# Sums of squares on VectorE in the first stage, and a reordered entry to the MLP

## The chip, the cores and the metric

The kernel runs on one core of a Trainium2 chip. Its five engines work beside each other, each through its own instructions in order: TensorE (PE; its weight loads are shown as PEld), VectorE (DVE), ScalarE (ACT), GpSimd (POOL) and SyncE (SP, which issues most DMAs). The metric is the device time of one execution in microseconds, as the median of several runs.

## The reference

One decoder layer over a sequence of 512 positions with a model width of 2048, in float32:

```python
a = rms_norm(h, norm_mix_pre)
z = a @ w_in          # recurrent branch, queries, keys, values, gates
y = concat([rms_norm(y_lru, gnorm_lru), rms_norm(y_nsa, gnorm_nsa)])
h = h + rms_norm(y @ w_out, norm_mix_post)
f = square(relu(rms_norm(h, norm_mlp_pre) @ mlp_w1)) @ mlp_w2
h = h + rms_norm(f, norm_mlp_post)
h = h + sigmoid(h @ ple_gate) * (p @ ple_proj)
```

The change touches two places: the first norm with the first products (the values and the gates), and the step from the mixer's output `h` into `mlp_w1`.

## The kernel before, in words

**Float32 products in three parts.** A matrix is split into a high part that TensorE multiplies exactly and a low part, the difference. ScalarE makes the high part and VectorE the low part, so each product is three matmuls (`mm3`): weight high with activation high, weight high with activation low, weight low with activation high. The weights come in strips of 128x512 (four tiles of 128x128). A strip's raw data lies in one of five `raw` buffers of two strips each, its high part is `shi` (ScalarE, L158) and its low part `slo` (VectorE, L159), in five buffers each. A raw buffer is free for SyncE's next load when its second `slo` is done. The activations' parts are `cx` or `cy`: two tiles (high, low) for each block of 128 channels.

**The order.** Work is a list of strips. `go()` walks through it: at strip j it fires the hooks of that place, splits strip j+4, and issues the 12 matmuls of strip j. `at(j, fn)` puts a hook at strip j, in quarters of a strip. So the order on every engine is written by hand, by the numbers in the tables, and each engine then waits for its data in that order. `store(dst, src, delay)` puts a DMA issue on ScalarE's queue `delay` strips later.

**The first stage** (`front`, 16 strips). Strip k holds the value weights of block k. For each of the 16 blocks of x, `x_step` splits the block (high on ScalarE and low on VectorE, L161 and L162), and `x_square` squares it on ScalarE (L601) and adds it into `msum`, on GpSimd (L605). At strip 6 `rms_a` reduces `msum` with 8 tiny matmuls on TensorE (L480) between strips 5 and 6. The gate weights are split into `gw` (L592, L593) ahead of block 1.

**The MLP's entry** (`back`). `b0` is the strip of four products of the last step (PLE), `bk = b0 + 4` the first of the MLP. The mixer's output lies in eight pairs `y[0]` to `y[7]` of two blocks each (128x1024). For pair i, `h1_a` multiplies by the norm and adds x (two VectorE instructions, L1432 and L1433), `h1_hi` makes the two high parts (ScalarE, L1440), `h1_lo` the two low parts (VectorE, L1443), `h1_sq` squares the pair into the tile that held x (ScalarE, L1449), `h1_add` adds the squares into `hs` (VectorE, L1453), which frees that tile for a later x, and `h1_e` scales the pair in place (ScalarE, L1456). `load_x` loads x for a pair; two tiles `xt` serve pairs 0, 1, 4, 5 and two tiles `xz` pairs 2, 3, 6, 7. The first four rows of `mlp_w1` run side by side (`add_plain`): 48 matmuls take blocks 0 to 3 for all four rows, then each row takes blocks 4 to 7 (one strip each), then 8 to 11, then 12 to 15. A pair's place is `b0 + HT[i]`, with its five steps at the offsets `HB`.

Of the kernel before, what the change touches and what calls it, by code (L numbers as in the profile page):

```python
# [11 lines left out]
AF = mybir.ActivationFunctionType  # L12
ALU = mybir.AluOpType
# [3 lines left out]
S = 512  # L17
# [17 lines left out]
NTAB = 1039  # L35
H = S // 2
PRIO = 20000
HT = (1.75, 2.75, 4, 4.25, 4.75, 8.5, 10.75, 12.25)
HB = (0, 0.5, 0.75, 1, 2)
HB1 = (0, 0.75, 1, 1.25, 2)  # L40
RMT = 16.5
WO = (-12, -7.75, -6.75, -5.75)
NPL = 12
# [60 lines left out]
GE = 8  # L104
# [18 lines left out]
def f32(ap):  # L123
    return ap.bitcast(F32)
# [14 lines left out]
class Build:  # L139
# [32 lines left out]
    def at(self, j, fn, *a):  # L172
        key = math.floor(4 * j + 0.5)
        assert self.now is None or key > self.now, (key, self.now)
        self.hooks.setdefault(key, []).append((fn, a))
# [385 lines left out]
    def front(self):  # L561
        nc, A, T, at = self.nc, self.A, self.T, self.at
        v, g, act, pe = nc.vector, nc.gpsimd, nc.scalar, nc.tensor
# [7 lines left out]
        gw = T["x2"].tile([P, KT, P], F32R, name="gw")  # L571
        sq_last = []
        wv = {}
# [6 lines left out]

        def load_wv(k):
            wv[k] = self.raw_tile()
            nc.sync.dma_start(wv[k], A["w_v"][k // 2])

        def load_gate():
            T["graw"] = self.raw_tile()
            nc.sync.dma_start(T["graw"][:, :768], A["w_gate"])
            g.memset(f32(gw), 0.0)

        def split_gate():  # L590
            src = T["graw"][:, :768].rearrange("p (k n) -> p k n", n=48)
# [7 lines left out]
        def x_square(k):  # L599
            sq = self.msum if k == 0 else T["x2"].tile([P, S], F32, tag="sq", name="sq", bufs=3)  # L600
            act.activation(sq, xs(k), AF.Square)  # L601
            if k == KT - 1:
                sq_last.append(sq)
            elif k:
                g.tensor_tensor(self.msum, self.msum, sq, op=ALU.add)  # L605

        def v_mm(j, q):
            if j == 0 and q == 0:
# [39 lines left out]


        self.msk = self.cp.tile([P, NB], F32, name="msk")  # L650
        at(-7, load_x, 0)
        at(-7, lambda: nc.sync.dma_start(self.vec, A["vecs"]))
        for i in range(8):
            at(-7 if i < 4 else 2 * i - 10, load_wv, 2 * i)
            if i == 0:
                at(-7, load_gate)
            for k in (2 * i + 1, 2 * i + 2):
                if k < KT:
                    at(-7 if i < 4 else -6, load_x, k)
# [3 lines left out]
        for k in range(KT):  # L663
            at(-3.75 + XS * (k - 1) if k else -5, x_step, k)
            at(XQ + XS * (k - 1), x_square, k)
            self.strips.append(Strip(lambda k=k: wv[k - k % 2][:, (k % 2) * 512:(k % 2 + 1) * 512], v_mm))
# [728 lines left out]
    def back(self):  # L1395
        nc, A, T, at = self.nc, self.A, self.T, self.at
        v, g, act = nc.vector, nc.gpsimd, nc.scalar
        V = self.vec

        b0 = len(self.strips)  # L1400
# [23 lines left out]
        def h1_a(i):  # L1424
            y, x, r = self.y[i], T["xt", i], T["Ro"]
            if i == 0:
                for a in range(2):
                    v.tensor_tensor(y[:, a], y[:, a], r, op=ALU.mult)
                    v.tensor_tensor(y[:, a], y[:, a], x[:, a], op=ALU.add)
                    h1_hi(a)  # L1430
            else:
                v.tensor_tensor(y, y, r.unsqueeze(1).to_broadcast([P, 2, S]), op=ALU.mult)  # L1432
                v.tensor_tensor(y, y, x, op=ALU.add)  # L1433
                if i > 1:
                    h1_hi(2 * i)
                    h1_hi(2 * i + 1)
            self.store(self.h1_d[2 * i:2 * i + 2].rearrange("a p n -> p a n"), y)

        def h1_hi(k):
            act.activation(up[k][:, 0], xs(k), AF.Copy, scale=V[:, V_MLPPRE + k:V_MLPPRE + k + 1])  # L1440
# [53 lines left out]
        bl = len(self.strips)  # L1494
        self.add_plain(bl, [A["mlp_w1"][m] for m in range(NPL - 4, NPL)], up, plain_a(NPL - 4), "Rm", (-8, -7, -6, -5))
        for i in range(KT // 2):
            j = b0 + HT[i]
            if i >= 4:
                at(b0 + HT[i - 4] + 2.25, load_x, 2 * i)
            if i == 1:  # L1500
                for a in range(2):
                    at(j + 0.5, h1_hi, 2 + a)
            for o, fn, k in zip(HB if i != 1 else HB1, (h1_a, h1_lo, h1_lo, h1_sq, h1_add), (i, 2 * i, 2 * i + 1, i, i)):
                at(j + o, fn, k)
            for a in range(2):
                at(j + GE, h1_e, 2 * i + a)
        at(bk + RMT, self.sqrt_table)
        at(bk + RMT, lambda: self.rms_a([T["hs"][:, 0], T["hs"][:, 1]], D, "m"))
        for i in range(KT // 2):
# [72 lines left out]
        for c in range(NCHUNK):  # L1582
            cb = len(self.strips)
            for k in range(FC):
                o = CU[k] if c == 0 else F1 + 4 * k if k < 8 else F2 + 0.4 * (k - 8)
# [80 lines left out]
        for i in range(KT // 2):  # L1666
            j = last + GT8[i]
# [109 lines left out]
```

## Time and profile before

| | |
|---|---|
| median of 3 runs | 2366.52 us (2366.48 to 2367.39) |
| the profiled execution's own time | 2364.17 us |
| its span in the trace | 2362.4 us |
| mean granted clock of TensorE | 0.997 |
| PE busy | 2316.7 us, 98% of the span |
| DVE, ACT, POOL busy | 59%, 44%, 5% |

The span runs from the first to the last instruction; 1.77 us of the profiled execution's time lie around it. The shares are means over stages with different limits; the two places of the change cover some 40 us and some 50 us of the span.

### The profile page before, as it was taken

The page shows a single profiled execution, that of the slowest core. Times are in us where ns is not written, and L with a number is a line of the kernel's source. Part 1 is how long each engine was busy: PE and PEld are TensorE (multiplying, and loading weights), DVE is VectorE, ACT ScalarE, POOL GpSimd, SP SyncE. Part 2 cuts the span into 40 slices and gives each one's busy share as a digit, 9 for nine tenths or more (in the row PEclk, how much of TensorE's full clock was granted, in tenths as well). Part 3 has the DMA queues.
Part 4 walks back from the last instruction along what each step waited for, and adds up shares of the span by engine and source line. Part 5 has one row for each costly group of instructions (what it writes and reads, how often), then busy time and mean ns, then how long its engine had stood idle before and what let it go on. Part 6 is the DMA issues. An engine that isn't in the chain of part 4 may idle for free.

```text
span 2362.4 us, 33256 instructions
## 1 busy us (share of the span) xinstructions
PE 2316.7 (98%) x12586; PEld 2004.2 (85%) x12586; DVE 1401.7 (59%) x2383; ACT 1039.6 (44%) x1927; POOL 108.5 (5%) x157
## 2 busy tenths in 40 slices
PE   7999999999999999999999999999999999999999
PEld 6788888787888778999999999888888888888887
DVE  6365665488746776888888888333333333334733
ACT  5354665387744563544444444333223223223422
POOL 4000000044410000000000000000000000000000
PEclk9999999999999999999999999999999999999999
DMA  5453232644234643433333335433333333224641
GB/s 190 155 179 121 96 110 103 174 124 122 99 116 134 234 149 107 143 132 130 128 130 127 134 125 184 155 116 134 116 116 132 110 115 134 98 99 134 221 145 69
DMA packets 113733, 315.59 MB, mean 134 GB/s; under 512 B 11459, under 2 KB 16835, under 8 KB 113573
## 3 DMA queue, kind: packets, MB, share of 16 engines
q1 hardware_dynamic: 94900, 275.13, 34.8%
q10 hardware_dynamic: 18672, 38.34, 4.6%
q8 instruction: 98, 1.61, 0.3%
q14 instruction: 63, 0.51, 0.1%
HBM read 270.37 MB, written 43.06 MB: 133 GB/s over the span
## 4 chain that ended last, share of the span: by engine, by line
PE 90%; DVE 4%; ACT 2%; DMA 2%; issue 1%; ACTq 0%; SPq 0%; POOL 0%; POOLq 0%; DVEq 0%
PE ps_mm L166 28%; PE ps_mm L168 27%; PE ps_mm L167 27%; PE ps_o L1301 1%; PE ps_t L1274 1%; DVE slo L159 1%; PE ps_s L1241 1%; DMA y<-in_xT_dram 1%; ACT shi L158 1%; PE ps_s L1242 0%; PE ps_mm L615 0%; ACT al_P L1254 0%; PE ps_mm L616 0%; PE ps_mm L614 0%; PE ps_t L480 0%
## 5 line engine op out<-in xcount | busy, mean ns | idle before, releaser
L159 DVE TENSOR_TENSOR slo<-raw,shi 128x512 fp32r<-128x512 f32 x808 | 558.7, 697 | 805.1 <-ACT shi L158 790.7
L158 ACT ACTIVATE shi<-raw 128x512 fp32r<-128x512 f32 x808 | 503.9, 629 | 912.9 <-PE ps_mm L167 804.6
L166 PE MATMUL ps_mm<-cx,shi 128*128 128x512 f32 (+1 forms) x1984 | 699.4, 353 | 3.8 <-ACT shi L158 1.9
L167 PE MATMUL ps_mm<-cx,shi 128*128 128x512 f32 (+1 forms) x1984 | 695.9, 351 | 3.4 <-DVE cx L1443 3.4
L168 PE MATMUL ps_mm<-cx,slo 128*128 128x512 f32 (+1 forms) x1984 | 696.1, 351 | 0.1
L166 PE MATMUL ps_mm<-cy,shi 128*128 128x512 f32 (+1 forms) x1536 | 544.0, 354 | 2.6 <-ACT shi L158 2.6
L167 PE MATMUL ps_mm<-cy,shi 128*128 128x512 f32 (+1 forms) x1536 | 543.3, 354 | 1.6 <-DVE cy L1443 1.6
L168 PE MATMUL ps_mm<-cy,slo 128*128 128x512 f32 (+1 forms) x1536 | 543.3, 354 | 0.6 <-DVE slo L159 0.6
L166 PEld LDWEIGHTS ps_mm<-cx,shi 128*128 128x128 f32 x1984 | 376.0, 189 | 52.6 <-ACT shi L158 3.1
L167 PEld LDWEIGHTS ps_mm<-cx,shi 128*128 128x128 f32 x1984 | 375.7, 189 | 51.8 <-DVE cx L1443 4.9
L168 PEld LDWEIGHTS ps_mm<-cx,slo 128*128 128x128 f32 x1984 | 375.5, 189 | 51.0 <-DVE slo L159 1.7
L166 PEld LDWEIGHTS ps_mm<-cy,shi 128*128 128x128 f32 x1536 | 290.8, 189 | 42.3 <-ACT shi L158 3.2
L167 PEld LDWEIGHTS ps_mm<-cy,shi 128*128 128x128 f32 x1536 | 290.9, 189 | 41.3 <-DVE cy L1443 2.4
L168 PEld LDWEIGHTS ps_mm<-cy,slo 128*128 128x128 f32 x1536 | 290.8, 189 | 41.0 <-DVE slo L159 1.2
L158 ACT ACTIVATE shi<-wsum 128x512 fp32r<-128x512 f32 x156 | 96.8, 628 | 124.0 <-PE ps_mm L167 73.4
L159 DVE TENSOR_TENSOR slo<-wsum,shi 128x512 fp32r<-128x512 f32 x156 | 106.3, 688 | 36.5 <-ACT shi L158 36.4
L1254 ACT ACTIVATE al_P<-al_P,ar_stm 128x512 f32<-128x512 f32 (+3 forms) x128 | 70.5, 555 | 13.7 <-DVE ar_stm L1249 13.3
L1264 POOL TENSOR_SCALAR al_P<-al_P,ar_sts 128x512 f32<-128x512 f32 (+3 forms) x128 | 71.9, 583 | 59.1 <-ACT al_ph L1286 28.7
L166 PE MATMUL ps_mm<-y,shi 128*128 128x256 f32 x208 | 58.3, 280 | 0.0
L167 PE MATMUL ps_mm<-y,shi 128*128 128x256 f32 x208 | 58.0, 279 | 0.0
L168 PE MATMUL ps_mm<-y,slo 128*128 128x256 f32 x208 | 58.0, 279 | 0.0
L1249 DVE CUSTOM_DVE_ANT_0 al_P<-ps_s,al_tb 128x512 f32<-128x512 f32 (+3 forms) x128 | 56.1, 483 | 2.7 <-POOL al_P L1264 1.6
(346 smaller groups left out, 1993.7 us busy)
## 6 DMA issues: line engine op xcount, KB each, us to landing
raw<-in_mlp_w_dram SPq DMA_DIRECT2D x256, 512.0 KB, 3.7
raw<-in_w_in_dram SPq DMA_DIRECT2D x64, 512.0 KB, 3.5
raw<-in_w_out_dram SPq DMA_DIRECT2D x32, 512.0 KB, 3.9
fk<-f_d SPq DMA_DIRECT2D x32, 512.0 KB, 4.9
raw<-in_ple_gate_dram SPq DMA_DIRECT2D x32, 512.0 KB, 4.1
f_d<-z ACTq DMA_DIRECT2D x26, 512.0 KB, 2.8
y<-in_xT_dram SPq DMA_DIRECT2D x16, 256.0 KB, 6.4
raw<-in_w_v_dram SPq DMA_DIRECT2D x8, 512.0 KB, 5.2
```

The lines of the kernel that those rows point to most:

```text
L158: nc.scalar.activation(hi, src, AF.Copy)
L159: (eng or nc.vector).tensor_tensor(lo, src, f32(hi), op=ALU.subtract)
L166: mm(ps, whi, ahi, start=start, stop=False)
L167: mm(ps, whi, alo, start=False, stop=False)
L168: mm(ps, wlo, ahi, start=False, stop=stop)
L1241: mm(ps[:, :n], lq, t["kh"][:, b, :n], start=True, stop=False)
L1249: v.tensor_tensor_reduce(out=PP[qt, b], in0=X["s", qt][b], in1=X["tb"][:, qt * P:], scale=1.0, scalar=3e38, op0=ALU.add, op1=ALU.min, accu ...
L1254: act.activation(PP[qt, b], PP[qt, b], AF.Exp, scale=-1.0, bias=st["mn"][:, qt, b:b + 1], accum_out=st["sm"][:, qt, b:b + 1])
L1264: pool.tensor_scalar(PP[qt, b], PP[qt, b], st["sm"][:, qt, b:b + 1], 1.0, op0=ALU.mult, op1=ALU.mult)
L1274: pe.transpose(pt[:, qt * P:(qt + 1) * P], PP[qt, b][:, kt * P:(kt + 1) * P], self.ident)
L1301: mm(po[:, :S - kt * P], vv[:, 0, b, :], y, start=False, stop=False)
```

## The change

In the first stage GpSimd's work goes away: the 14 adds into `msum` and the clearing of `gw` go to VectorE. A one-element activation is put ahead of ScalarE's first work. The first load of value weights is issued as two halves. At the MLP's entry each step of each pair has a table of its own (`HA_` for `h1_a`, `HH_` for the high parts, `HL_` for the low parts, `HS_` for the squares, `HD_` for their sums, `HX_` for the loads of x), in place of one place for each pair and common offsets; the stores of `h1` stay one strip behind, the fifth pair's one and a half.

```diff
-HT = (1.75, 2.75, 4, 4.25, 4.75, 8.5, 10.75, 12.25)
-HB = (0, 0.5, 0.75, 1, 2)
-HB1 = (0, 0.75, 1, 1.25, 2)
+HA_ = (1.75, 2.75, 3.75, 4.5, 4.75, 8.5, 10.5, 12.25)
+HH_ = (0, 3.25, 4.25, 4.75, 5.25, 9.25, 11.25, 13.25)
+HL_ = (2.25, 3.5, 4.25, 4.75, 5.5, 9.5, 11.5, 13.5)
+HS_ = (2.75, 4.25, 4.75, 5.25, 6.5, 10.25, 12.25, 14.25)
+HD_ = (0, 4.75, 6.25, 7.25, 14.5, 15, 15.5, 16)
+HX_ = (0, 0, 0, 0, 2.25, 5, 6.5, 7.5)
...
         def load_wv(k):
             wv[k] = self.raw_tile()
-            nc.sync.dma_start(wv[k], A["w_v"][k // 2])
+            for c in (slice(0, S), slice(S, 2 * S)) if k == 0 else (slice(0, 2 * S),):
+                nc.sync.dma_start(wv[k][:, c], A["w_v"][k // 2][:, c])
...
-            g.memset(f32(gw), 0.0)
...
-                g.tensor_tensor(self.msum, self.msum, sq, op=ALU.add)
+                v.tensor_tensor(self.msum, self.msum, sq, op=ALU.add)
...
+        act.activation(self.scrap, self.ones, AF.Copy)
+        v.memset(f32(gw), 0.0)
...
-                if i > 1:
-                    h1_hi(2 * i)
-                    h1_hi(2 * i + 1)
-            self.store(self.h1_d[2 * i:2 * i + 2].rearrange("a p n -> p a n"), y)
+            self.store(self.h1_d[2 * i:2 * i + 2].rearrange("a p n -> p a n"), y, 1 if i != 4 else 1.5)
...
         for i in range(KT // 2):
-            j = b0 + HT[i]
             if i >= 4:
-                at(b0 + HT[i - 4] + 2.25, load_x, 2 * i)
-            if i == 1:
-                for a in range(2):
-                    at(j + 0.5, h1_hi, 2 + a)
-            for o, fn, k in zip(HB if i != 1 else HB1, (h1_a, h1_lo, h1_lo, h1_sq, h1_add), (i, 2 * i, 2 * i + 1, i, i)):
-                at(j + o, fn, k)
+                at(b0 + HX_[i], load_x, 2 * i)
             for a in range(2):
-                at(j + GE, h1_e, 2 * i + a)
+                if i:
+                    at(b0 + HH_[i], h1_hi, 2 * i + a)
+                at(b0 + HL_[i] + (0.25 if i == 0 else 0) * a, h1_lo, 2 * i + a)
+                at(b0 + max(HA_[i] + GE, 15 if i > 4 else 0), h1_e, 2 * i + a)
+            at(b0 + HA_[i], h1_a, i)
+            at(b0 + HS_[i], h1_sq, i)
+            if i:
+                at(b0 + HD_[i], h1_add, i)
```

TensorE's instructions and their order are the same in both kernels. Three places show what moves on the engines that it waits for.

VectorE in the first stage before, from block 1's low part on (`cy` is the activation's low part, `slo` the strip's; the second, third and fourth `slo` are those of strips 1, 2 and 3):

```order
L162 SCALAR_TENSOR_TENSOR cy_104<-y0_95,vec_61,cy_104 128x512
L162 SCALAR_TENSOR_TENSOR cy_105<-y1_96,vec_61,cy_105 128x512
L159 TENSOR_TENSOR slo_169<-raw_123,shi_168 128x512
L162 SCALAR_TENSOR_TENSOR cy_106<-y1_96,vec_61,cy_106 128x512
L162 SCALAR_TENSOR_TENSOR cy_107<-y2_97,vec_61,cy_107 128x512
L162 SCALAR_TENSOR_TENSOR cy_108<-y2_97,vec_61,cy_108 128x512
L159 TENSOR_TENSOR slo_192<-raw_130,shi_191 128x512
```

The same stretch of VectorE in the changed kernel, up to strip 2's low part:

```order
L165 SCALAR_TENSOR_TENSOR cy_104<-y0_95,vec_61,cy_104 128x512
L608 TENSOR_TENSOR msum_66<-msum_66,sq_162 128x512
L165 SCALAR_TENSOR_TENSOR cy_105<-y1_96,vec_61,cy_105 128x512
L608 TENSOR_TENSOR msum_66<-msum_66,sq_167 128x512
L162 TENSOR_TENSOR slo_171<-raw_125,shi_170 128x512
L165 SCALAR_TENSOR_TENSOR cy_106<-y1_96,vec_61,cy_106 128x512
L608 TENSOR_TENSOR msum_66<-msum_66,sq_176 128x512
L165 SCALAR_TENSOR_TENSOR cy_107<-y2_97,vec_61,cy_107 128x512
L608 TENSOR_TENSOR msum_66<-msum_66,sq_181 128x512
L165 SCALAR_TENSOR_TENSOR cy_108<-y2_97,vec_61,cy_108 128x512
L608 TENSOR_TENSOR msum_66<-msum_66,sq_190 128x512
L162 TENSOR_TENSOR slo_194<-raw_132,shi_193 128x512
```

An add into `msum` now stands behind every block's low part, so each strip's low part has two or three more instructions ahead of it.

ScalarE at the MLP's entry before, from pair 2's high parts on (`y2_` to `y4_` are the pairs, `shi` a strip's high part, `ppo` an output of the PLE product, `xz` a square):

```order
L1440 ACTIVATE cy_7388<-y2_6705,vec_61 128x512
L1440 ACTIVATE cy_7389<-y2_6705,vec_61 128x512
L158 ACTIVATE shi_7538<-raw_7276 128x512
L1387 ACTIVATE ppo_7542<-ps_mm_7512 128x512
L1387 ACTIVATE ppo_7542<-ps_mm_7522 128x512
L1440 ACTIVATE cx_7390<-y3_6706,vec_61 128x512
L1440 ACTIVATE cx_7391<-y3_6706,vec_61 128x512
L1440 ACTIVATE cx_7392<-y4_6707,vec_61 128x512
L1440 ACTIVATE cx_7393<-y4_6707,vec_61 128x512
L1449 ACTIVATE xz_7412<-y2_6705 128x1024
L422 DMA h1_d_75<-y2_6705 128x2x512
L158 ACTIVATE shi_7617<-raw_7306 128x512
```

The same stretch of ScalarE in the changed kernel, from pair 2's high parts to the strip behind pair 4's:

```order
L1442 ACTIVATE cy_7390<-y2_6707,vec_61 128x512
L1442 ACTIVATE cy_7391<-y2_6707,vec_61 128x512
L1451 ACTIVATE xz_7414<-y2_6707 128x1024
L1442 ACTIVATE cx_7392<-y3_6708,vec_61 128x512
L1442 ACTIVATE cx_7393<-y3_6708,vec_61 128x512
L425 DMA h1_d_75<-y2_6707 128x2x512
L161 ACTIVATE shi_7617<-raw_7308 128x512
L1451 ACTIVATE xz_7416<-y3_6708 128x1024
L1442 ACTIVATE cx_7394<-y4_6709,vec_61 128x512
L1442 ACTIVATE cx_7395<-y4_6709,vec_61 128x512
L425 DMA h1_d_75<-y3_6708 128x2x512
L161 ACTIVATE shi_7629<-raw_7330 128x512
```

The high part of the second weight row's strip (`shi_7617`) now stands ahead of pair 4's high parts (the fifth pair's); the first row's strip and the last PLE output have moved ahead of pair 2, outside this piece.

VectorE at the MLP's entry before, from pair 3's update on:

```order
L1432 TENSOR_TENSOR y3_6706<-y3_6706,ps_t_7457 128x1024
L1433 TENSOR_TENSOR y3_6706<-y3_6706,xz_7414 128x1024
L1443 SCALAR_TENSOR_TENSOR cy_7388<-y2_6705,vec_61,cy_7388 128x512
L1453 TENSOR_TENSOR hs_7499<-hs_7499,xt_7316 128x1024
L1443 SCALAR_TENSOR_TENSOR cy_7389<-y2_6705,vec_61,cy_7389 128x512
L1443 SCALAR_TENSOR_TENSOR cx_7390<-y3_6706,vec_61,cx_7390 128x512
L1432 TENSOR_TENSOR y4_6707<-y4_6707,ps_t_7457 128x1024
L1433 TENSOR_TENSOR y4_6707<-y4_6707,xt_7536 128x1024
L1443 SCALAR_TENSOR_TENSOR cx_7391<-y3_6706,vec_61,cx_7391 128x512
L159 TENSOR_TENSOR slo_7618<-raw_7306,shi_7617 128x512
```

The same stretch of VectorE in the changed kernel:

```order
L1445 SCALAR_TENSOR_TENSOR cy_7390<-y2_6707,vec_61,cy_7390 128x512
L1445 SCALAR_TENSOR_TENSOR cy_7391<-y2_6707,vec_61,cy_7391 128x512
L1437 TENSOR_TENSOR y3_6708<-y3_6708,ps_t_7459 128x1024
L1438 TENSOR_TENSOR y3_6708<-y3_6708,xz_7416 128x1024
L1455 TENSOR_TENSOR hs_7503<-hs_7503,xt_7318 128x1024
L1445 SCALAR_TENSOR_TENSOR cx_7392<-y3_6708,vec_61,cx_7392 128x512
L1445 SCALAR_TENSOR_TENSOR cx_7393<-y3_6708,vec_61,cx_7393 128x512
L1437 TENSOR_TENSOR y4_6709<-y4_6709,ps_t_7459 128x1024
L1438 TENSOR_TENSOR y4_6709<-y4_6709,xt_7493 128x1024
L162 TENSOR_TENSOR slo_7618<-raw_7308,shi_7617 128x512
```

Each pair's two low parts now stand ahead of the next pair's update. Further back, the sums of squares of pairs 4 to 7 have moved behind pair 7's low parts.

## Rows read from the trace of the kernel before

**Rows 1.** The page's busy time, share of the span and instructions, by engine.

```profile
PE 2316.7 (98%) x12586; PEld 2004.2 (85%) x12586; DVE 1401.7 (59%) x2383; ACT 1039.6 (44%) x1927; POOL 108.5 (5%) x157
```

**Rows 2.** One stretch: its us, busy PE, PEld, DVE, ACT, POOL; clock, DMA share, GB/s.

```profile
30.00:34.00 4.00, 3.03 (x13) 2.53 (x14) 4.00 (x3) 1.55 (x3) 3.61 (x3) 1.00 0.01 2
```

**Rows 3.** Timeline of the first stage, VectorE and GpSimd: start, duration, instruction.

```profile
9.86 2.44 DVE L162 SCALAR_TENSOR_TENSOR cy<-y,vec,cy 128x512 fp32r<-128x512 f32 x2
10.17 23.60 POOL L605 TENSOR_TENSOR msum<-msum,sq 128x512 f32<-128x512 f32 x14 [7.64 <-ACT sq L601]
...
13.93 5.16 DVE L162 SCALAR_TENSOR_TENSOR cy<-y,vec,cy 128x512 fp32r<-128x512 f32 x3
...
34.24 0.68 DVE L159 TENSOR_TENSOR slo<-raw,shi 128x512 fp32r<-128x512 f32 x1
...
34.85 2.06 DVE L162 SCALAR_TENSOR_TENSOR cx<-y,vec,cx 128x512 fp32r<-128x512 f32 x3
```

**Rows 4.** Timeline of the first stage: the gate's load (SPq), ScalarE's start.

```profile
2.12 0.43 SPq L587 DMA_DIRECT2D raw<-in_w_gate_dram  x1
...
3.72 1.28 ACT L161 ACT_TABLE_LOAD   x1 [3.72 <-DMA vec<-in_vecs_dram]
...
8.11 0.84 ACT L592 ACTIVATE gw<-raw 128x768 fp32r<-128x768 f32 x1 [0.61 <-DMA raw<-in_w_gate_dram]
```

**Rows 5.** Timeline of the first stage, TensorE: second matmuls of strips 1, 2, 5, and after.

```profile
14.06 0.50 PE L615 MATMUL ps_mm<-slo,cy 128*128 128x512 f32 x1 [0.57 <-DVE slo L159]
...
20.81 0.50 PE L615 MATMUL ps_mm<-slo,cy 128*128 128x512 f32 x1 [3.29 <-DVE slo L159]
...
34.98 0.50 PE L615 MATMUL ps_mm<-slo,cy 128*128 128x512 f32 x1 [0.54 <-DVE slo L159]
...
38.06 0.28 PE L480 MATMUL ps_t<-ones,msum 128*128 128x1 f32 x2
...
39.77 0.48 PE L614 MATMUL ps_mm<-shi,cy 128*128 128x512 f32 x1
```

**Rows 6.** Timeline of TensorE at the MLP's entry.

```profile
809.32 0.39 PE L166 MATMUL ps_mm<-cy,shi 128*128 128x512 f32 x1
810.45 0.50 PE L167 MATMUL ps_mm<-cy,shi 128*128 128x512 f32 x1 [0.74 <-DVE cy L1443]
...
815.96 0.49 PE L167 MATMUL ps_mm<-cx,shi 128*128 128x512 f32 x1 [2.03 <-DVE cx L1443]
...
818.13 0.79 PE L166 MATMUL ps_mm<-cy,shi 128*128 128x512 f32 x1 [1.44 <-ACT shi L158]
...
831.77 0.40 PE L166 MATMUL ps_mm<-cx,shi 128*128 128x512 f32 x1
...
837.01 0.39 PE L168 MATMUL ps_mm<-cx,slo 128*128 128x512 f32 x1
...
847.57 0.50 PE L166 MATMUL ps_mm<-cx,shi 128*128 128x512 f32 x1
```

**Rows 7.** Timeline of VectorE at the MLP's entry.

```profile
803.50 1.22 DVE L1433 TENSOR_TENSOR y<-y,xz 128x1024 f32<-128x1024 f32 x1
806.65 0.69 DVE L159 TENSOR_TENSOR slo<-raw,shi 128x512 fp32r<-128x512 f32 x1 [1.93 <-ACT shi L158]
...
809.65 0.74 DVE L1443 SCALAR_TENSOR_TENSOR cy<-y,vec,cy 128x512 fp32r<-128x512 f32 x1
...
815.16 0.74 DVE L1443 SCALAR_TENSOR_TENSOR cx<-y,vec,cx 128x512 fp32r<-128x512 f32 x1
```

**Rows 8.** Timeline of ScalarE at the MLP's entry.

```profile
815.28 0.72 ACT L1440 ACTIVATE cx<-y,vec 128x512 fp32r<-128x512 f32 x1 [4.18 <-DVE y L1433]
...
816.52 1.04 ACT L1449 ACTIVATE xz<-y 128x1024 f32<-128x1024 f32 x1
817.47 0.61 ACT L158 ACTIVATE shi<-raw 128x512 fp32r<-128x512 f32 x1
...
839.44 1.32 ACT L1456 ACTIVATE y<-y,vec 128x512 f32<-128x512 f32 x2
```

## The prediction

> **What bounds the kernel now.** I read the page's busy shares first: TensorE works 98% of the span [rows 1], so the time is its work plus the stretches in which it waits, and a change that leaves its instructions alone can only take or add waits. The list of who waits for whom sends me to two places, the first 40 us and the MLP's entry, and I read both in the timelines, engine by engine.
>
> In the first stage TensorE waits for the strips' low parts, 0.57 us at strip 1, 3.29 at strip 2, 0.54 at strip 5 [rows 5]. VectorE makes them and has no gap. It is slow: three low parts of blocks take 5.16 us, 1.72 each, while GpSimd adds into `msum` from 10.17 to 33.77; as soon as GpSimd is done, three of the same take 2.06 us [rows 3]. GpSimd is the cause, not the loads: from 30 to 34 us the DMA share is 0.01 and VectorE still finishes three instructions in 4 us [rows 2].
>
> At the MLP's entry TensorE waits for the pairs' parts and for the strips. From 831.77 to 837.01 it issues 24 matmuls without a wait, 0.228 us apart. From 809.32 to 847.57 lie 108 issues (48 on blocks 4 to 7, 48 on 8 to 11, 12 on 12 to 15), which at that pace are 24.6 us; they take 38.25 [rows 6]. So 13.6 us are lost there. That is the ceiling of what an order can win at the entry.
>
> **The first stage, step by step.** Alone, VectorE starts a block's low part every 0.66 us ((2.06 - 0.74)/2; a single one lasts 0.74) and, behind a subtraction, the next instruction after 0.61 (34.24 to 34.85) [rows 3, 7]. The trace has no add of `msum` on VectorE. From below it costs 0.61, the pace of a subtraction of the same size; from above 1.69, the pace under GpSimd (1.72 less the tail of the last). I take 0.61, since GpSimd has nothing to do there any more. The chain starts at 9.86 as before, for the gate's split in front of it ends on a load (8.11) that the change doesn't hasten [rows 3, 4]. Adding up the new order (two block parts, two adds, `slo`; then three, three, `slo`; two, two, `slo`, three times; three, three, `slo`; one, `slo`) gives the ends of strips 1 to 7's low parts: 13.1, 17.5, 20.7, 23.8, 27.0, 31.4, 32.7. ScalarE's inputs are earlier everywhere, since it no longer waits for GpSimd to free a square.
>
> TensorE follows. From a strip's second matmul to the next strip's it needs 3.31 us (34.98 to 38.06 is 3.08, and one issue of 0.23) [rows 5]. Strip 1's second matmul goes at 13.15, strip 2's could at 16.46 and waits until 17.57, strips 3, 4, 5 go at 20.9, 24.2, 27.5 without a wait. The 8 reductions could start at 30.58, and the last add into `msum` ends at 30.8, so 30.83. Strip 6 starts 1.71 later, as before (38.06 to 39.77): 32.54 in place of 39.77, **7.2 us won**. Behind it the low part of strip 7 is there at 32.7 for 36.
>
> What else is in this stage costs nothing: the clearing of `gw` takes VectorE from nothing to at most the time of four subtractions (four times the elements), 2.7 us, at its start, where none of its inputs is there before 3.72, when ScalarE's first data lands [rows 4]. The early activation pulls the table load (1.28 us at 3.72) [rows 4] ahead of the first data; it brings up to 1.28 us for the first parts, which the gate's load takes back. The halved first load lets TensorE begin some tenths sooner, and strip 1's low part takes this back too; it puts one more issue (0.43 us) ahead of the gate's load [rows 4], so the term is 7.2 or, with that load 0.43 later, 6.8.
>
> **The entry, step by step.** Everything is the same up to pair 2's update, which ends at 804.72 [rows 7]. The first row's strip is now split ahead of that, so its low part no longer waits for ScalarE (1.93 us) [rows 7], and the low parts of blocks 4 and 5 follow at once, done at 806.3 and 806.9, where the first was done at 810.4 [rows 7]. The waits at them (the 0.74 of 810.45 is the first [rows 6]) go. An instruction on a whole pair lasts 1.22 [rows 7]; I count 1.25 where the next one needs its result and 1.14 where not, with the 0.08 of overlap that the block parts show (0.74 to 0.66). Pair 3's update takes 1.25 + 1.22 to 809.3, a sum of squares 1.14, then blocks 6 and 7 end at 811.1 and 811.8. TensorE comes to block 6 at 810.7: 0.25 us of wait there and none at block 7, where 2.03 were [rows 6].
>
> It reaches the second row at 812.4. Its high part was at 817.47, behind pair 4's parts (815.28) and a square [rows 8]; now it stands ahead of them, done at 811.2. What is late next is its low part, on VectorE behind pair 4's update: 811.7 + 2.5 = 814.1, and 0.69 for itself. The third matmul waits from 812.9 to 814.8, **1.9 us**. The next two rows' low parts end at 817.0 and 818.7 and are needed at 817.6 and 820.3. Pair 5's update is reached at 820.4, since its turn comes behind four strips' low parts and two sums; block 10 is done at 824.4, 0.3 late. Pair 6 is done at 831, three us early. Pair 7's update ends at 835.25, but ScalarE's queue then holds two pairs scaled in place (four activations, 0.6 apart) [rows 8] and a strip ahead of its high parts, so these end at 836.7 and the low parts at 837.4 and 838.1; TensorE is there at 835.3 and waits 1.5 and 0.55 us. With 0.1 us for each restart the waits come to 4.9 us, where 13.6 were: the second row's blocks 12 to 15 start at 838.8, not 847.57, **8.8 us won**.
>
> The queues it moves past: SyncE issues pair 4's x ahead of two stores, and the x tiles of pairs 6 and 7 come free at 818.1 and 819.8, behind the sums of squares, for use at 827.8 and 834.0; a load has 10 us there. The sums of pairs 4 to 7, now last, end at 844.1; the reduction that needs them comes behind two more rows and a strip, at 849. The stores of `h1` wait for updates that are done.
>
> The bounds of this term: nothing less than 13.6 - 4.9 if every instruction keeps its duration and no wait is missed. If the clock falls once as at 818.13, where a matmul takes 0.79 and others after a wait 0.50 [rows 6], the lower of the two levels (1.2 for 2.4 GHz) adds 0.228 us to each matmul, 1.4 to six of them; if pair 7's scalings find their turn late and the low parts of two pairs slip by a strip (2.7 us), the term is 5. From above, if all but the 1.9 is hidden, 11.
>
> **A rule that speaks against it.** VectorE is full in the first stage (4.00 of 4.00 us) [rows 2], and the change gives it 14 more instructions. The Trainium skill, Perfetto Trace Analysis, Optimizing Scalar/DVE Operations, says that where VectorE is saturated, moving work to ScalarE or even GpSimd may help, and adds that GpSimd shares a read port with it, so it might not. By its first half the 14 adds would lengthen the queue by 14 x 0.61 = 8.5 us and the change would lose there; by the rows a pace of 1.7 goes to 0.6 and the queue shortens. The trace agrees with the second half.
>
> **Rivals.** *The entry gives less*: one of the pairs' chains slips by a strip, or the clock falls: 7.2 + 5 won, 2354.3. For it speaks that ScalarE's and VectorE's queues there are added up from many durations; against it, that none of them changes. *The first stage gives less*: the gate's load comes much later than I think, or loads hold the blocks. With half of the 7.2, 2354.1. *The waits move on*, to work behind the entry, and less than 4.7 us remain: about 2364. Against it: TensorE's order is the same and what it waits for later hangs on work that moves with it. *Slower*: the slow pace isn't GpSimd's doing but that of these instructions in this stage, and stays at 1.69. Then 34 instructions (14 block parts, 14 adds, 6 low parts) end at 9.86 + 57.5 = 67.3, strip 6 starts 27.6 us later than now, and with 8.8 won the time is 2385. This decides from a pace of 1.14 us on (9.86 + 34 x 1.14 = 39.77 + 8.8). Against it: the pace changes within one instruction of GpSimd's end [rows 3].
>
> **How the numbers follow.** 7.2 + 8.8 = 16.0 us. The profiled execution's own time, 2364.17, has 1.77 around its span and would be 2348.2. The median of the runs shown is 2366.52, 2.35 above that execution, so I forecast 2350.5. Chances: the forecast, 2346 to 2353.5, 74 in 100; the entry gives less, 11; the first stage gives less, 9; the waits move on, 4; slower, 2. The range 2346 to 2356.5 takes in the two smaller gains. A measurement of this kernel can tell about 0.2% (4.7 us): faster by more than that 0.94, within it 0.04, slower 0.02.
>
> **What would show it.** Right: no GpSimd work before the attention; VectorE's `slo` instructions in the first stage 0.69 long, strip 2's wait near 1.1 us and strip 6's first matmul near 32.5; at the entry, with all times about 7 us earlier than my numbers, one wait of about 1.9 us at the second row's third matmul and one of about 2 at block 14, none at blocks 4 and 5. Wrong: instructions of VectorE still near 1.7 us in the first stage; the gate's split later than 9; a third large wait at the entry, for a load of x or for pair 5.

## The result, and the profile after

The changed kernel takes 2351.49 us (median of 6 runs, 2349.10 to 2353.67) where the kernel before takes 2366.50 (6 runs): a ratio of 0.9936 with a 95% interval of 0.9926 to 0.9946, 15.0 us less. The profiled execution took 2352.03 us, its span is 2350.2.

TensorE's work is the same, and the span is 12.2 us shorter; the page's first line, which answers to [rows 1], shows POOL 24 us lighter and DVE no heavier, though it has taken over 15 of POOL's instructions:

```profile
PE 2316.3 (99%) x12586; PEld 2006.0 (85%) x12586; DVE 1397.3 (59%) x2398; ACT 1039.8 (44%) x1928; POOL 84.2 (4%) x142
```

**The first stage.** VectorE's timeline in the changed kernel, which answers to [rows 3] (start, duration, instruction, and in brackets the idle time before it and who ended it; L165 is a block's low part, L608 an add into `msum`, L162 a strip's low part):

```profile
1.23 1.76 DVE L655 MEMSET gw<- 128x2048 f32 x1 [1.23 <-PEq L1775]
...
10.04 0.75 DVE L165 SCALAR_TENSOR_TENSOR cy<-y,vec,cy 128x512 fp32r<-128x512 f32 x1
10.70 0.68 DVE L608 TENSOR_TENSOR msum<-msum,sq 128x512 f32<-128x512 f32 x1
...
16.36 0.68 DVE L608 TENSOR_TENSOR msum<-msum,sq 128x512 f32<-128x512 f32 x1
16.96 0.68 DVE L162 TENSOR_TENSOR slo<-raw,shi 128x512 fp32r<-128x512 f32 x1
...
30.16 0.68 DVE L608 TENSOR_TENSOR msum<-msum,sq 128x512 f32<-128x512 f32 x1
```

An add lasts 0.68 us and the next instruction starts 0.60 after it; block parts are back at 0.74, where they took 1.72 [rows 3]. ScalarE's side answers to [rows 4]: the gate's weights arrive 0.18 later (8.29 in place of 8.11), so the chain starts at 10.04 and not at 9.86.

```profile
8.29 0.84 ACT L595 ACTIVATE gw<-raw 128x768 fp32r<-128x768 f32 x1 [2.00 <-DMA raw<-in_w_gate_dram]
```

TensorE's timeline there answers to [rows 5]. The kernel before had a fourth wait for a strip's low part, 1.62 us at strip 4, which the prediction's list leaves out. It also had a stretch at the lower clock in this stage, from 22.3 to 25.7, but that cost nothing: the next low part, strip 3's, was done only at 25.84, and TensorE took it at 25.89. From the kernel before, VectorE and TensorE:

```profile
24.07 1.77 DVE L159 TENSOR_TENSOR slo<-raw,shi 128x512 fp32r<-128x512 f32 x1
```

```profile
25.89 0.50 PE L615 MATMUL ps_mm<-slo,cy 128*128 128x512 f32 x1
...
30.97 0.50 PE L615 MATMUL ps_mm<-slo,cy 128*128 128x512 f32 x1 [1.62 <-DVE slo L159]
```

In the changed kernel two of these waits are left, 0.84 at strip 1 and 0.93 at strip 2; the reductions wait 0.37 for the last add, and strip 6 starts at 32.70 in place of 39.77:

```profile
13.31 0.50 PE L618 MATMUL ps_mm<-slo,cy 128*128 128x512 f32 x1 [0.84 <-DVE slo L162]
...
17.70 0.50 PE L618 MATMUL ps_mm<-slo,cy 128*128 128x512 f32 x1 [0.93 <-DVE slo L162]
...
30.89 0.38 PE L483 MATMUL ps_t<-ones,msum 128*128 128x1 f32 x2 [0.37 <-DVE msum L608]
...
32.70 0.48 PE L617 MATMUL ps_mm<-shi,cy 128*128 128x512 f32 x1
```

**The MLP's entry.** TensorE's timeline, which answers to [rows 6], from the first row's block 4 (804.81) to the second row's block 12 (835.15):

```profile
804.81 0.39 PE L169 MATMUL ps_mm<-cy,shi 128*128 128x512 f32 x1
...
806.68 0.50 PE L170 MATMUL ps_mm<-cx,shi 128*128 128x512 f32 x1
...
808.18 0.39 PE L170 MATMUL ps_mm<-cy,shi 128*128 128x512 f32 x1
810.33 0.50 PE L171 MATMUL ps_mm<-cy,slo 128*128 128x512 f32 x1 [1.76 <-DVE slo L162]
...
819.95 0.50 PE L170 MATMUL ps_mm<-cx,shi 128*128 128x512 f32 x1
...
830.55 0.39 PE L171 MATMUL ps_mm<-cx,slo 128*128 128x512 f32 x1
832.30 0.50 PE L169 MATMUL ps_mm<-cx,shi 128*128 128x512 f32 x1 [1.36 <-ACT cx L1442]
833.08 0.57 PE L170 MATMUL ps_mm<-cx,shi 128*128 128x512 f32 x1 [0.28 <-DVE cx L1445]
833.45 0.63 PE L171 MATMUL ps_mm<-cx,slo 128*128 128x512 f32 x1
833.87 0.63 PE L169 MATMUL ps_mm<-cx,shi 128*128 128x512 f32 x1
...
835.15 0.63 PE L169 MATMUL ps_mm<-cx,shi 128*128 128x512 f32 x1
```

Between the same two matmuls the kernel before took 38.25 us; here it is 30.34, 7.9 less. What is left of waits: 0.28 at block 6, 1.92 at the second row's third matmul (810.33 less 808.18, less an issue of 0.23), 0.19 at block 10, and at block 14 1.52 for the high and 0.55 for the low part. Then the matmuls come 0.43 apart instead of 0.23: the granted clock has fallen to its lower level behind the two waits, and eight matmuls pay 0.2 each, four of them up to block 12. The kernel before had a fall in this stretch too, behind 818.13 [rows 6]: to 821.15 seven issues take 3.02 us where 1.60 is their pace, and with 0.1 for the restart the fall took 1.3 us. So the waits alone, with their restarts, went from 12.3 us (13.6 less 1.3) to 4.9 (30.34 less 24.6 for the 108 issues, less 0.8).

Who is late at block 14 is seen on ScalarE and VectorE. Pair 7's update ends at 830.82, but ScalarE is still scaling two pairs in place (four activations, 2.55 us) and then splits a strip; pair 7's high parts start at 831.54:

```profile
828.57 2.55 ACT L1458 ACTIVATE y<-y,vec 128x512 f32<-128x512 f32 x4
...
831.02 0.61 ACT L161 ACTIVATE shi<-raw 128x512 fp32r<-128x512 f32 x1
831.54 1.32 ACT L1442 ACTIVATE cx<-y,vec 128x512 fp32r<-128x512 f32 x2
```

```profile
829.60 1.22 DVE L1438 TENSOR_TENSOR y<-y,xz 128x1024 f32<-128x1024 f32 x1
831.66 0.69 DVE L162 TENSOR_TENSOR slo<-raw,shi 128x512 fp32r<-128x512 f32 x1 [0.84 <-ACT shi L161]
832.28 1.41 DVE L1445 SCALAR_TENSOR_TENSOR cx<-y,vec,cx 128x512 fp32r<-128x512 f32 x2
```

**Where the rest went.** I cut each trace into four parts: up to strip 6's first matmul; the middle, up to the first matmul behind the reduction of the mixer's output; the entry, up to the first matmul behind the eight tiny ones of the MLP's norm; and the rest, which is 1503.1 to 1503.2 us in every trace but that of e6_scale_late (1504.6, with a fall of the clock at 941). What tells the other twelve apart lies in the first three parts. "Clock" is what the lower level took: 10 us times one minus the granted clock, summed over 10-us windows counted from the part's start. One fall mostly counts 1.7 there; where TensorE was waiting during part of it, it cost less.

| kernel | median us | ratio to before (95%) | strip 6 at | middle (clock) | entry (clock) |
|---|---|---|---|---|---|
| before | 2366.50 | | 39.77 | 751.6 (1.7) | 67.8 (1.7) |
| after | 2351.49 | 0.9936 (0.9926 to 0.9946) | 32.70 | 754.2 (5.1) | 60.3 (1.7) |
| e1_stage | 2360.20 | 0.9973 (0.9961 to 0.9984) | 32.38 | 754.4 (5.1) | 67.8 (3.4) |
| e2_entry | 2358.59 | 0.9968 (0.9955 to 0.9980) | 39.59 | 752.8 (3.4) | 60.3 (1.7) |
| e3_adds | 2359.58 | 0.9973 (0.9964 to 0.9982) | 32.71 | 753.2 (3.4) | 68.7 (3.4) |
| e4_extras | 2367.59 | 1.0005 (0.9996 to 1.0014) | 39.91 | 754.9 (5.1) | 67.8 (3.4) |
| e5_gp_reads | 2361.25 | 0.9978 (0.9968 to 0.9987) | 44.06 | 750.7 (1.7) | 60.3 (1.7) |
| e5_gp_writes | 2352.89 | 0.9940 (0.9927 to 0.9952) | 32.85 | 755.6 (6.8) | 60.3 (1.7) |
| e6_scale_late | 2350.15 | 0.9928 (0.9916 to 0.9940) | 32.80 | 753.2 (3.4) | 58.0 (0) |
| e7_pair4_first | 2349.94 | 0.9931 (0.9917 to 0.9944) | 33.07 | 754.3 (5.1) | 60.5 (1.7) |
| e8_again | 2352.43 | 0.9945 (0.9932 to 0.9959) | 33.14 | 756.1 (6.8) | 60.3 (1.7) |
| e9_scale_spread | 2347.99 | 0.9929 (0.9916 to 0.9941) | 32.62 | 751.6 (1.7) | 57.7 (1.7) |
| e10_spread_pair4 | 2353.69 | 0.9949 (0.9937 to 0.9962) | 32.87 | 757.2 (8.5) | 59.7 (1.7) |

The profiled execution won 7.1 in the first stage and 7.6 at the entry, and lost 2.6 in the middle, which the change doesn't touch. There its clock is lower in two places more than before's. Three windows of the changed kernel (busy us of PE, PEld, DVE, ACT, POOL, then the granted clock, DMA share, GB/s), with the one that answers to [rows 2] ahead:

```profile
30.00:34.00 4.00, 3.63 (x25) 2.99 (x24) 3.59 (x11) 0.98 (x3) 0.00 (x0) 1.00 0.08 22
...
150.00:160.00 10.00, 10.00 (x48) 8.42 (x47) 7.29 (x18) 6.45 (x14) 0.00 (x0) 0.83 0.39 135
...
460.00:470.00 10.00, 7.77 (x28) 5.86 (x29) 5.03 (x15) 2.57 (x4) 0.00 (x0) 0.83 0.50 150
...
640.00:650.00 10.00, 10.00 (x55) 8.72 (x54) 6.47 (x17) 5.98 (x17) 4.10 (x8) 0.89 0.16 58
```

In the kernel before, the same windows show 1.00, 1.00 and 0.83. Both kernels wait at all three places, for 1.7 to 3.2 us (the first is 3.19 us at 156.76 before and 2.94 at 149.38 after), so the length of the wait alone doesn't decide whether the clock falls.

### The profile page after: what moved, and what is told of

Read it like the earlier page. It is cut to its first block, busy times and chain, and to the rows that moved or that the text cites. A ratio compares the mean times of both kernels' runs of the same rounds, so it can differ in the third digit from the quotient of the medians.

```text
span 2350.2 us, 33252 instructions
## 1 busy us (share of the span) xinstructions
PE 2316.3 (99%) x12586; PEld 2006.0 (85%) x12586; DVE 1397.3 (59%) x2398; ACT 1039.8 (44%) x1928; POOL 84.2 (4%) x142
## 4 chain that ended last, share of the span: by engine, by line
PE 91%; DVE 4%; ACT 3%; DMA 1%; issue 1%; SPq 0%; ACTq 0%; POOL 0%; POOLq 0%; DVEq 0%
PE ps_mm L169 28%; PE ps_mm L171 28%; PE ps_mm L170 28%; PE ps_o L1306 1%; PE ps_t L1279 1%; DVE slo L162 1%; ACT shi L161 1%; PE ps_s L1246 1%; PE ps_s L1247 0%; ACT al_P L1259 0%; PE ps_t L483 0%; PE ps_mm L617 0%; PE ps_mm L619 0%; PE ps_mm L618 0%; DVE y L1438 0%
## 5 line engine op out<-in xcount | busy, mean ns | idle before, releaser
L162 DVE TENSOR_TENSOR slo<-raw,shi 128x512 fp32r<-128x512 f32 x808 | 554.3, 691 | 797.1 <-ACT shi L161 782.7
L162 DVE TENSOR_TENSOR slo<-wsum,shi 128x512 fp32r<-128x512 f32 x156 | 106.1, 687 | 36.8 <-ACT shi L161 36.7
```

What stands on the lines that cost most here:

```text
L162: (eng or nc.vector).tensor_tensor(lo, src, f32(hi), op=ALU.subtract)
```

## The experiments

**e1_stage and e2_entry: each half alone.** The first takes only these lines of the diff, the second all the others:

```diff
-            nc.sync.dma_start(wv[k], A["w_v"][k // 2])
+            for c in (slice(0, S), slice(S, 2 * S)) if k == 0 else (slice(0, 2 * S),):
+                nc.sync.dma_start(wv[k][:, c], A["w_v"][k // 2][:, c])
-            g.memset(f32(gw), 0.0)
-                g.tensor_tensor(self.msum, self.msum, sq, op=ALU.add)
+                v.tensor_tensor(self.msum, self.msum, sq, op=ALU.add)
+        act.activation(self.scrap, self.ones, AF.Copy)
+        v.memset(f32(gw), 0.0)
```

> The first stage's edits alone, the MLP's entry as before. My account (two independent terms): strip 6's first matmul near 32.7 us in place of 39.77, so 7.1 us won, about 2359.4; at the MLP's entry all of the old waits, 13.6 us. The rival, that the entry carries nearly all of the gain: under 3 us won, above 2363.

> The MLP entry's edits alone, the first stage as before, with GpSimd's adds. My account: 8.8 us won, less some 1.5 where the clock falls, so 2357.7 to 2359.5; strip 6's first matmul at 39.8; at the entry one wait of 1.8 us at the second row's third matmul and one of some 1.7 at block 14. The rival, that the first stage carries nearly all: under 3 us won.

Against the kernel before on the same chip (2366.18) the first won 6.0 us and the second 7.6. In the traces the first moves strip 6 to 32.38 and leaves the entry at 67.8; the second leaves strip 6 at 39.59 and has the changed kernel's entry, with its two waits (1.76 at the second row, 1.35 at block 14). Each half leaves the other's place as it was, and 13.6 for both is near the 15.0 of the change.

**e3_adds and e4_extras: the first stage taken apart.** The first moves only the 14 adds; the second does the rest of the stage's edits and leaves the adds on GpSimd.

```diff
-                g.tensor_tensor(self.msum, self.msum, sq, op=ALU.add)
+                v.tensor_tensor(self.msum, self.msum, sq, op=ALU.add)
```

> Only the 14 adds go from GpSimd to VectorE; the clearing of gw stays on GpSimd, no early activation, the first load in one piece. My account: VectorE's low parts 0.74 and 0.68 us long throughout, strip 6's first matmul between 32.4 and 32.8, 7.1 us won, 2359.4. The rival, that the earlier start (table load, half load) is needed too: one to two us less won, strip 6 near 34.

> The early activation, the load in halves and the clearing on VectorE, with the adds left on GpSimd. My account: TensorE begins near 6.3 instead of 7.6, and the time stays within 1 us of before (2366.5), since strip 1's low part waits for the gate's load and for VectorE at 1.7 us an instruction. The rival, that an earlier start is carried through: 1.2 us or more won.

The adds alone bring strip 6 to 32.71, and 6.6 us in the time; the other edits bring nothing that can be measured (e4_extras' median is 1.4 above before's on that chip, where I had said within 1, but its interval includes a ratio of 1). With the adds still on GpSimd VectorE stays slow, as e4_extras' timeline shows (three block parts in 5.16 us, a low part in 1.76):

```profile
12.38 1.76 DVE L159 TENSOR_TENSOR slo<-raw,shi 128x512 fp32r<-128x512 f32 x1
14.07 5.16 DVE L162 SCALAR_TENSOR_TENSOR cy<-y,vec,cy 128x512 fp32r<-128x512 f32 x3
```

**e5_gp_reads and e5_gp_writes: is it GpSimd's presence, or its reading?** To the changed kernel comes work on a tile that nobody uses, in the first 14 adds of GpSimd, which last 22.7 us in all, in the second 40 clearings, which last 23.3:

```diff
+        idle = self.sum_tile("idle")
+        g.memset(idle, 0.0)
+        for _ in range(14):
+            g.tensor_tensor(idle[:, :S], idle[:, :S], idle[:, S:], op=ALU.add)
```

```diff
+        idle = self.sum_tile("idle")
+        for _ in range(40):
+            g.memset(idle[:, :S], 0.0)
```

> The changed kernel with 14 adds of 128x512 on GpSimd over an unused tile, on which nothing waits. If reads by GpSimd hold VectorE up, the chain of msum having no part in it: about half of the adds run before 10 us, the rest at 1.7 us each beside VectorE's until some 22 us, VectorE's instructions are 1.6 to 1.8 us long until then, strip 6 starts near 40, and the time is 6 to 9 us above the changed kernel's. If it was the chain through msum (ScalarE waiting for GpSimd, GpSimd for ScalarE): VectorE at 0.7, the time of the changed kernel.

> The changed kernel with 40 clearings of an unused 128x512 tile on GpSimd from the start on, which only write. If GpSimd's reads are what holds VectorE up: VectorE's instructions stay at 0.68 to 0.75 us, strip 6's first matmul near 32.7, the time that of the changed kernel (2351.5, within 1.5). If any work of GpSimd holds it up: some of VectorE's instructions beyond 1 us, strip 6 after 35, 2354 or more.

Timelines of e5_gp_reads, GpSimd's and VectorE's: while GpSimd adds, VectorE's add takes 1.76 us, and the first instruction after it 0.74.

```profile
1.77 22.73 POOL L659 TENSOR_TENSOR idle<-idle 128x512 f32<-128x512 f32 x14
```

```profile
23.29 1.76 DVE L608 TENSOR_TENSOR msum<-msum,sq 128x512 f32<-128x512 f32 x1
24.97 0.74 DVE L165 SCALAR_TENSOR_TENSOR cy<-y,vec,cy 128x512 fp32r<-128x512 f32 x1
25.63 0.68 DVE L608 TENSOR_TENSOR msum<-msum,sq 128x512 f32<-128x512 f32 x1
```

The same two of e5_gp_writes: GpSimd is as busy, and VectorE keeps its pace.

```profile
0.73 23.28 POOL L658 MEMSET idle<- 128x512 f32 x40 [0.29 <-POOLq L1778]
```

```profile
10.19 0.75 DVE L165 SCALAR_TENSOR_TENSOR cy<-y,vec,cy 128x512 fp32r<-128x512 f32 x1
10.85 0.69 DVE L608 TENSOR_TENSOR msum<-msum,sq 128x512 f32<-128x512 f32 x1
```

So the slow pace comes with GpSimd's adds and not with its clearings, for VectorE's adds and parts alike, with no data passing between the two engines. The Trainium skill, SBUF — State Buffer, Who interferes with whom, says this: a VectorE instruction with two inputs in SBUF contends with a GpSimd instruction that reads SBUF, and not with one that only writes it. The trace agrees, with 1.76 against 0.69. An add differs from a clearing in more than its reading, but the middle part of the changed kernel speaks for the reading too. There GpSimd scales tiles in SBUF, one input each, and VectorE's subtraction of a strip, whose two inputs lie in SBUF, takes 1.02 beside it; the instructions ahead of it and behind it, one input of which is a `ps_` tile of TensorE's result memory (PSUM), keep to 0.69 and 0.68:

```profile
570.32 4.53 POOL L1269 TENSOR_SCALAR al_P<-al_P,ar_sts 128x512 f32<-128x512 f32 x8 [3.19 <-ACT al_ph L1291]
```

```profile
571.97 0.69 DVE L1295 TENSOR_TENSOR al_pl<-ps_t,al_ph 128x512 fp32r<-128x512 f32 x1
572.57 1.02 DVE L162 TENSOR_TENSOR slo<-raw,shi 128x512 fp32r<-128x512 f32 x1
573.51 0.68 DVE L1016 TENSOR_TENSOR z<-ps_mm,rl 128x512 f32<-128x512 f32 x1
```

The price was larger in e5_gp_reads than I expected: strip 6 came at 44.06 and not near 40. VectorE is only 9.3 us later than in the changed kernel (24.97 for the block part that starts at 15.70 there); the other 2 are TensorE's, which behind a wait of 3.10 us ran at the lower clock (0.67 from 20 to 30 us).

**e6_scale_late and e9_scale_spread: block 14's wait.** The scalings of pairs 2 to 4 move behind pair 7's high parts, first all to one place, then one pair between two strips:

```diff
-                at(b0 + max(HA_[i] + GE, 15 if i > 4 else 0), h1_e, 2 * i + a)
+                at(b0 + max(HA_[i] + GE, 15 if i > 4 else 14 if i > 1 else 0), h1_e, 2 * i + a)
```

```diff
-                at(b0 + max(HA_[i] + GE, 15 if i > 4 else 0), h1_e, 2 * i + a)
+                at(b0 + max(HA_[i] + GE, (0, 0, 14, 14.75, 15.5, 15, 15, 15)[i]), h1_e, 2 * i + a)
```

> The changed kernel with the in-place scalings of pairs 2, 3 and 4 behind pair 7's high parts on ScalarE. If these scalings hold up pair 7, as I read it: pair 7's high parts start when its update ends, the wait at block 14 goes from 1.36 us to under 0.7, and 1 to 2 us are won against the changed kernel, more where a fall of the clock behind that wait goes too. If VectorE's queue is what is late: the wait stays above 1.2 and the time is the same.

> The changed kernel with the in-place scalings of pairs 2, 3 and 4 at 14, 14.75 and 15.5, one pair between two strips. Theory (block 14's wait is ScalarE's queue ahead of pair 7's high parts, and the first try lost 1.1 us because six scalings in one piece held the next strips' high parts): the wait at block 14 is at most 0.3, as there, and VectorE's next low part of a strip no longer waits 3.4 us for ScalarE; the entry takes 56.9 to 57.6 us (57.99 in the first try, 60.26 in the changed kernel with a clock fall of 1.7), the time is 0.5 to 1.5 below the first try's and 1.5 to 3 below the changed kernel's. Rival (the 1.1 us come from somewhere else): the entry is 58.0 again.

In both the wait for block 14's high part is gone; in e6_scale_late that is the scalings' doing alone, while in e9_scale_spread TensorE also comes there later, after a fall of the clock at the second row. In e6_scale_late six scalings run in one piece from 830.16 for 3.78 us, and VectorE's next strip waits behind them:

```profile
834.50 0.69 DVE L162 TENSOR_TENSOR slo<-raw,shi 128x512 fp32r<-128x512 f32 x1 [3.40 <-ACT shi L161]
```

Spread, that wait is 0.94 in e9_scale_spread:

```profile
830.28 0.69 DVE L162 TENSOR_TENSOR slo<-raw,shi 128x512 fp32r<-128x512 f32 x1 [0.94 <-ACT shi L161]
```

The entry fell to 57.7 with a clock fall in it, 2.5 us below the changed kernel's with one. That is just above the range I gave, whose upper end left no room for a fall. At 2347.99 it has the lowest median of all; beside the changed kernel on the same chip (2352.43) it is 4.4 us lower, more than the 1.5 to 3 that I gave; the entry gives 2.5 of it, and the rest is no more than the clock in the middle makes from run to run. The two intervals overlap by a little.

**e7_pair4_first and e10_spread_pair4: the fifth pair.** Its high parts go ahead of the second row's strip again, first in the changed kernel, then in e9_scale_spread:

```diff
-HH_ = (0, 3.25, 4.25, 4.75, 5.25, 9.25, 11.25, 13.25)
+HH_ = (0, 3.25, 4.25, 4.75, 5, 9.25, 11.25, 13.25)
```

> The changed kernel with pair 4's high parts (the fifth pair's) ahead of the second row's strip again, everything else kept. My account: the strip's high part ends some 4.9 us later than in the changed kernel, behind pair 4's update; TensorE waits at the second row's first matmul, and its low part comes some 2 us later, so 2 us are lost against the changed kernel. The rival, that the low part waits for VectorE behind pair 4's update in any case: no loss.

> The kernel with spread scalings, and the fifth pair's high parts ahead of the second row's strip again. Theory (putting the fifth pair behind the strip was worth nothing in the changed kernel because the time it won at the second row was lost again at block 14; with block 14's wait gone it is worth its own 2 us): the second row's first matmul waits about 3.5 us in place of 1.76 at the third, nothing is given back at block 14, and the entry takes 1.5 to 2.2 us more than with the spread scalings alone. Rival (the edit is worth nothing by itself): the entries of the two agree to 0.5 us.

I had it wrong for the first. TensorE's timeline of e7_pair4_first shows why: the second row waits 3.49 us at its first matmul, some 2 us more than 1.76 at the third, as I said; but at block 14 the wait of 1.36 is gone, for pair 7 comes when it came and TensorE comes later.

```profile
812.09 0.50 PE L169 MATMUL ps_mm<-cy,shi 128*128 128x512 f32 x1 [3.49 <-ACT shi L161]
...
835.30 0.50 PE L170 MATMUL ps_mm<-cx,shi 128*128 128x512 f32 x1 [0.28 <-DVE cx L1445]
```

The entry is 60.5 against 60.3. With block 14's wait gone anyway the same edit is worth its 2 us: e10_spread_pair4 waits 3.50 at the second row and gives nothing back, 59.7 against e9_scale_spread's 57.7, each with one clock fall.

```profile
814.75 0.50 PE L169 MATMUL ps_mm<-cy,shi 128*128 128x512 f32 x1 [3.50 <-ACT shi L161]
```

Its median is 5.7 higher, more than that; its middle is 5.6 longer in the profile and shows 8.5 us of lower clock, where e9_scale_spread's shows 1.7.

**e8_again: the changed kernel a second time.**

> The changed kernel once more, unaltered: a second profile of it, and its time beside the other two. Theory (the clock's falls in the middle part, 2.6 us there and 1.7 at the entry, belong to one execution and not to the change): the instructions' order and the waits at the first stage and the entry are the same to 0.1 us, strip 6 begins at 32.5 to 32.9, but the places of the falls differ from the first profile's (151, 465, 639, 833) in at least one, and the middle part lies anywhere from 750.5 to 755.5 us. Rival (the change itself causes them, through the earlier arrival): the falls come at the same four places with the same 7, 5, 3 and 8 matmuls, and the middle part is 754.2 again.

Strip 6 comes 0.4 us later than in the first profile, at 33.14, just above the range I gave: the gate's weights arrive 0.44 later (ScalarE starts on them at 8.73), and VectorE's chain behind them is later by as much. The entry agrees to 0.1. The falls don't all come at the same places: none at 150 now, new ones at 34, just behind strip 6's start and so in the middle, and at 530, and again those at 460, 640 and 830. Its windows:

```profile
30.00:40.00 10.00, 9.59 (x44) 7.71 (x43) 8.83 (x33) 4.68 (x10) 0.00 (x0) 0.83 0.29 94
...
150.00:160.00 10.00, 8.58 (x50) 7.54 (x50) 8.54 (x20) 7.56 (x17) 0.00 (x0) 1.00 0.50 156
...
460.00:470.00 10.00, 7.72 (x28) 5.38 (x27) 4.76 (x13) 1.84 (x2) 0.00 (x0) 0.83 0.54 173
530.00:540.00 10.00, 9.00 (x41) 7.94 (x42) 7.63 (x25) 5.66 (x17) 5.89 (x9) 0.83 0.68 162
640.00:650.00 10.00, 9.00 (x42) 7.78 (x43) 6.92 (x24) 5.01 (x17) 4.10 (x8) 0.83 0.14 50
```

The middle, 756.1, is above the range I gave. With the clock taken off, the thirteen middles of the table lie between 748.6 and 749.9, before's at 749.9 and the two of the changed kernel at 749.1 and 749.2, so its instructions and waits there are not slower. That the falls belong to single executions is shown for 34, 150 and 530; those at 460 and 640 came in both profiles, and whether the earlier arrival makes these two likelier is open: two profiles don't tell. Over whole executions the runs show no loss: the mean granted clock of the changed kernel's eleven runs (the result's six and these five) is 0.9970 on average, that of the 44 runs of the kernel before beside the experiments 0.9958; on this chip alone it is 0.9968 against 0.9963. The profiled execution of before, at 0.997, is among that kernel's highest.

## Why the prediction was right

**The pace of VectorE alone.** The step on which the first term hung holds: adds start the next instruction 0.60 after them, as subtractions do. Strip 6 came at 32.70 for 32.54, 7.07 won for 7.2; the 0.16 is the gate's load, which came 0.18 later, inside the 0.43 that I had set aside for it. Whether the halved first load did that is not shown: the split of the gate's weights starts at 7.94 to 8.30 in the three profiles with the load in one piece and at 7.97 to 8.73 in the ten with halves. That the adds do it alone and the other edits nothing is shown by e3_adds and e4_extras. The rival *Slower* is out: the pace is GpSimd's doing (e5_gp_reads), and more exactly that of its reading, as far as clearings, which leave the pace alone, and the one-input scalings tell.

**The entry's waits.** I gave 0.25, 1.9, 0.3, 1.5 and 0.55; they are 0.28, 1.92, 0.19, 1.52 and 0.55, so adding up durations queue by queue was good to 0.1 us. The term of 8.8 measured 7.9 up to the second row's block 12: block 14's two waits were followed by a fall of the clock, 0.8 us up to that matmul and 1.6 in all. I had named such a fall as a bound (1.4) and left it out of the sum, although the 13.6 that I started from held one of 1.3, which I so counted as won. The 4.9 that I gave for the waits is what the trace shows.

**The sum.** 16.0 forecast, 15.0 between the medians, 12.2 between the two profiled executions; 2350.5 forecast, 2351.49 measured. In the profiles the two places gave 7.1 and 7.6, and the middle took 2.6 back, with 3.4 us more of lower clock than in before's. That is the chance of these two executions: over the runs the changed kernel's granted clock is no lower than before's (e8_again), and *The waits move on* is not what happened. The sum has no term for the clock over the whole execution, which moves single runs by several us, so that the medians came within 1.0 of it is partly luck.

**What I took for part of the gain and isn't.** I read the second row's strip ahead of pair 4's high parts as part of the 8.8. In this kernel that edit is worth nothing: what it wins at the second row is lost at block 14, where pair 7's end sets the time. The total was right because I followed the chain up to block 14, and a price put on that edit alone would have been 2 us too high.

## What to carry to other kernels

Before work is given to GpSimd to spare VectorE, look at VectorE's durations while GpSimd reads: here 14 adds of GpSimd cost VectorE about 1 us for each of its own instructions meanwhile, more than doing the adds itself (0.6), while clearing tiles on GpSimd was free. In a chain with two waits, as at the entry, an edit at the first is worth nothing while the second is set by something that doesn't move; price edits at the last wait of the chain, and remove that one first. Move a long row of cheap activations out of the way one at a time, between the work that others wait for, not in one piece.

## What the runs showed of the hardware

That a wait of TensorE can cost more than itself, and not each time: a wait of 1.3 to 3.8 us was followed by some eight matmuls 0.43 apart (the lower level, 1.2 GHz, where 0.23 is the pace at the upper) in some executions and not in others, up to 1.7 us each, and in a few places for twice as long (0.66 from 150 to 160 us in e10_spread_pair4). Nor did every fall come right behind a long wait: in four of the thirteen profiles (e6, e8, e9 and e10) the clock fell at 33 to 34 us, just behind the first stage's reduction (1.8 us of tiny matmuls), before which TensorE had waited 0.4 us; in the changed kernel's first profile it did not fall there, behind the same work. The wait of 1.76 at the second row had no fall behind it in the changed kernel, and had one behind 1.77 us in e9_scale_spread (from 807.68 on). In the middle part alone the lower clock took 1.7 to 8.5 us of a profile, more than several edits of this study are worth. The runs of one kernel spread with it: of the changed kernel's second set the fastest, 2350.84 us, had a mean granted clock of 0.998, and the slowest, 2354.36, one of 0.996, and 0.002 of the time is 4.7 us.
